# A hybrid attention and expert-retrieval layer on one core: gate rows two units later, a low half ahead of the norm's constants, and another order of loads, copies and factors where the dense experts change stage

## The chip, the cores and the metric

The kernel runs on one core of one Trainium2 chip. The metric is the device time in microseconds of one execution. Before the change the median of three runs is 1756.65 us (1754.71 to 1765.33). Engines are named as the profile names them: PE is TensorE (matrix products), PEld its weight loads, DVE is VectorE, ACT is ScalarE, POOL is GpSimd, SP is SyncE, which here only issues transfers.

## What is computed

One decoder layer on 512 tokens of 1024 features, in float32. The first part is the mixer, the second an expert layer that retrieves 16 of 16384 single-neuron experts for each token and each of 8 heads.

```python
h = rmsnorm(x, norm_mix_g)
proj = h @ w_in                       # all branches at once
o_a = gla_chunked(gq, gk, gv, log_a)  # gated linear attention
o_a = rmsnorm(o_a, gla_norm_g) * silu(gr)
o_b = swa_sink_attention(q, k, sv, attn_sinks)   # window 128, sinks
merged = sigmoid(gate_a) * (o_a @ w_branch_a) + sigmoid(gate_b) * (o_b @ w_branch_b)
x = x + merged @ w_out
xn = rmsnorm(x, norm_ffn_g)
# product keys: top 16 of 128 on each side, top 16 of their sums -> idx, gate (softmax)
out = x + sum_k gate[k] * gelu(peer_u[idx[k]] . xn) * peer_v[idx[k]]
```

## The kernel before

**Weights come as units.** A stream (class Stream, L124 to L183) brings one 128 x 1024 float32 block at a time: SyncE loads it (`raw`, L143), ScalarE makes a rounded high half (`whi`, L162), VectorE or GpSimd makes the low half (`wlo`, L172). Each product is three matmuls (high by high, high by low, low by high), at L231 and L248 in the first part. The first two blocks are split in halves of 512 columns (`first`, L154 and L155) between the rows of the first norm's input (L270 to L276); the third is split by the first call of `get`, which stands behind the constants of the attention (masks and scaled gains, L306 to L330).

**The front.** Units of the mixer follow one another: keys and values of the window attention, queries, then eight units `gr` (swish gate of branch A, L609 to L626) and eight units `gb`. The window attention itself runs as a side generator, one step each few matmuls of the units (`swa`, L428 to L515): scores on TensorE, masks and maxima on VectorE, exponentials on ScalarE, then transposes, and two masked copies `pc` and `pp` (L475, L479) that the products `o_` (L489) read. In the gate units, `gr_act(d)` (L600) puts a tanh of row d on a list that the next attention step hands to ScalarE (L601), and `gr_late` (L604) at the end of the next unit issues the product of that row on VectorE (L609). Row 3 is the first for which this is done in its own unit; rows 0, 1 and 2 are handled together with rows 3, 4 and 5.

**The dense experts.** Instead of gathering, 368 of the 512 tokens go through all 16384 experts, 128 per unit, in three stages of 92, 20 and 16 units (PHASES, L79; main loop L1529 to L1591). Each stage has an up part and a down part. In the up part, `h_step` (L1375) multiplies a block of U into a PSUM bank `hp` (24 matmuls at L231) and ScalarE writes its gelu (L1393) into `ring` or, where it is spilled to memory, `hw`. In the down part, `v_step` multiplies blocks of V into eight accumulators (L1445). Its other operand is the gelu times a gate tile: `w_a` (L1419) multiplies ring and gate tile `gt` on VectorE (`wr`, L1424) and rounds on ScalarE (`wh`, L1429); `w_b` (L1432) makes the low half (`wl`, L1435). The first pair of a stage is made before the last up unit, together with the first half of the second pair. The gate tiles are loaded by `g_load` (L1408) in two pieces: `gd`, built with one-hot matmuls during the first up part, and `g3`, into which 128 scatters of GpSimd (L1143) add the gates of one quarter of the tokens. The first two `g_load` of the kernel are issued by GpSimd in unit 86, the others by SyncE.

**The rest of the tokens.** 144 tokens are handled by gathering rows of U and V: GpSimd gathers one row per token (L1310), VectorE makes the product with the token (L1325), ScalarE its gelu and gate (L1281, L1282), VectorE adds the scaled row of V (L1342). This is a generator (`gather`, L1287); `pump` (L1478) advances it when the planner's counters `pe`, `dve`, `dma` and `pool`, which add a cost per instruction issued, leave room. Up to unit 83 it uses single row buffers ("early"); after `late[0]` is set it uses the pair buffers of the gate builder, and the activation of a row is issued right behind its product. In unit 86 the early rows are used up (L1545), the memory of the routing stage is closed, and the gate loads are issued.

**Banks.** PSUM has eight banks: S2 (two), PT, O, M0 to M3. BANKS (L1527) says which accumulator lies where; up units from 92 on alternate between M0 and M1. Between a down part and the next up part, `sum_phase` (L1490) copies accumulators 7 and 6 on ScalarE (L1502 in the first, L1499 in the second) and leaves the others to the following up units.

The order on every engine is the order in the program: each engine works through its own instructions in turn and waits on semaphores.

Of the kernel before, what the change touches and what calls it, by code (L numbers as in the profile page):

```python
# [47 lines left out]
N0 = 92  # L48
# [4 lines left out]
TAIL = 5  # L53
SLACK = 3.0
DUTY = 0.97
LAND = 10.0
POOLQ = 9.0
# [26 lines left out]
def tile_block(ctx, tc, xT, wst, smalls, wgk2, keysT, uT, vv, uv_rows, out):  # L84
# [186 lines left out]
    for kb in range(KB):  # L271
        g = S("gmix")[:, kb:kb + 1]
        nc.scalar.activation(hhi[:, kb], xt[:, kb], AF.Copy, scale=g)
        nc.vector.scalar_tensor_tensor(hlo[:, kb], xt[:, kb], g, hhi[:, kb].bitcast(F32), OP.mult, OP.subtract)
        if kb < 4:
            st.first(kb // 2, kb % 2)  # L276
    xs = Bt[:, 0]
    rb = F.tile([128, T], F32, name="rb", tag="rb")
    rt = F.tile([128, 4, NT], F32, name="rt")[:, 0:2]
# [320 lines left out]
    def gr_act(d):  # L600
        fill.append(lambda: nc.scalar.activation(gb[:, d], gr[:, d], AF.Tanh, scale=0.5))  # L601
        late.append(d)
# [8 lines left out]
    for d in range(8):  # L611
        w = unit("gr")
        if d == NR:
            flush()
            gb = F.tile([128, KB, T], F32, name="gb", tag="gb")
            side.append(swa())
            nm[0] = 3
            st.defer = True
        ps = proj(w, H, each=tick)
        nc.vector.tensor_tensor(gr[:, d], ps, rb, OP.mult)  # L620
        gr_late()
        if d >= NR:
            gr_act(d)
            if d < 2 * NR:
                gr_act(d - NR)
    for d in range(8):  # L626
        w = unit("gb")
        zero_fill()
# [638 lines left out]
            yield  # L1267

    late, early, used, acc2 = [False], [0], [-1], []
    nxt, born, end, en = [], {}, [False], [0]  # L1270
    sel = XP.tile([128, XG], F32, name="sel")
    nc.gpsimd.tensor_tensor(sel, ident[:, 0:XG], ident[:, XG:2 * XG], OP.add)
# [14 lines left out]
    def gather():  # L1287
# [7 lines left out]

        def issue(k):
            nonlocal grp, n
            while n < min(n_, k + (3 if late[0] else 2) + 2 * end[0]):
                for i in range(min(2 if late[0] else 1, n_ - n)):
                    if late[0]:  # L1300
                        if i == 0:
# [47 lines left out]

        issue(0)  # L1350
        pu, pv = 0, 0
        nxt[:] = [0]
        yield
        while pv < n_:
# [123 lines left out]
    def pump():  # L1478
        for x in (dve, dma, pool):
            x[0] = max(x[0], pe[0] - SLACK)  # L1480
        for _ in range(2):
            if side and max(dve[0], dma[0], pool[0] - (0 if late[0] else POOLQ)) < pe[0] + SLACK:
                if nxt and not late[0] and pe[0] < born[nxt[0]] + LAND:
                    break
                u = used[0]
                step()
                if used[0] > u:
                    break
# [35 lines left out]
                    nc.sync.dma_start(out[(t + 1) * 128 - n:(t + 1) * 128, ch], xr[0:n, t, ch])  # L1524
        return tr

    BANKS = ("S2", "S2", "PT", "O", "M2", "M3", "M0", "M1")  # L1527
    b_s = NB
    for ph, (b0, b1) in enumerate(PHASES):  # L1529
        for b in range(b0, b1):  # L1530
            if b == b1 - 1:
                w_a(b0 // 2)
                w_b(b0 // 2)
                w_a(b0 // 2 + 1)
            h_step(b, feed if LEAD <= b < N0 - GL else None)
            if b == RS[0]:
# [2 lines left out]
                next(r_)  # L1539
            if b == RS[-1]:  # L1540
                side.append(gather())
            if b == N0 - TAIL - 4:
                late[0] = True
            if b == N0 - TAIL - 1:
                while early[0]:  # L1545
                    step()
# [3 lines left out]
            if b == N0 - GL:  # L1550
                assert next(r_, 0) == 0
                while gout:
                    gout.pop(0)()
                g_load(0, nc.gpsimd)
                g_load(1, nc.gpsimd)
            pool[0] = max(pool[0], pe[0] - SLACK)
            if scs:
                b_s = min(b_s, b)
# [13 lines left out]
        for b in range(b0, b1 - 2 if last else b1):  # L1572
# [8 lines left out]
            if b % 2 == 0 and p + 1 < b1 // 2:  # L1581
                w_b(p + 1)
            v_step(b, b == b0, b == b1 - 1)
            pump()
            if b == NB - 6:
                xr = P.tile([128, 4, D], F32, name="xr", tag="hhi")
                nc.sync.dma_start(xr[0:TB, 1], x1s[XG:, 1])
                nc.sync.dma_start(xr[0:XG, 0], x1s[0:XG, 1])
                nc.sync.dma_start(xr[:, 2:4], x1s[:, 2:4])
        if not last:  # L1590
            sum_phase(ph)  # L1591
    wl_ = [get("V", NB - 2), get("V", NB - 1)]
    trs = []
    for c in range(7, -1, -1):
# [89 lines left out]
```

## Time and profile before

| what | value |
|---|---|
| runs (three), median | 1756.65 us |
| lowest, highest | 1754.71, 1765.33 us |
| profiled execution, its own time | 1764.95 us |
| its span, first to last instruction | 1763.0 us |
| mean granted clock of TensorE | 0.992 |
| HBM read, written | 379.67 MB, 42.47 MB |
| first up part begins, ends (PE) | 647.5, 1080.8 us |
| first down part begins, ends | 1083.9, 1455.5 us |
| second up part begins; second down part | 1460.1; 1542.4 us |
| third up part begins; third down part | 1622.9; 1687.5 us |

The profile is one execution. Its rows give a start in us from the span's start, a duration in us, the engine, the line, the operation and its operands (out<-in), and in brackets the idle time before it and what ended it. In the view of waits a row gives an engine's line, whom it waited for, the total, the number of times and the longest. In the view of windows the columns are PE, PEld, DVE, ACT and POOL busy time with instruction counts, then granted clock, DMA share and GB/s.

### The profile page before, as it was taken

The page shows a single profiled execution, that of the slowest core. Times are in us where ns is not written, and L with a number is a line of the kernel's source. Part 1 is how long each engine was busy: PE and PEld are TensorE (multiplying, and loading weights), DVE is VectorE, ACT ScalarE, POOL GpSimd, SP SyncE. Part 2 cuts the span into 40 slices and gives each one's busy share as a digit, 9 for nine tenths or more (in the row PEclk, how much of TensorE's full clock was granted, in tenths as well). Part 3 has the DMA queues.
Part 4 walks back from the last instruction along what each step waited for, and adds up shares of the span by engine and source line. Part 5 has one row for each costly group of instructions (what it writes and reads, how often), then busy time and mean ns, then how long its engine had stood idle before and what let it go on. Part 6 is the DMA issues. An engine that isn't in the chain of part 4 may idle for free.

```text
span 1763.0 us, 26377 instructions
## 1 busy us (share of the span) xinstructions
PE 1724.8 (98%) x9866; PEld 1599.9 (91%) x9866; DVE 1304.9 (74%) x2547; ACT 765.9 (43%) x1334; POOL 705.9 (40%) x447
## 2 busy tenths in 40 slices
PE   9999999999998999999999999999999998999998
PEld 7776688988886889999999989999999998999998
DVE  7767624346337996977778746999889998899874
ACT  5545523335244234355555533444444434444441
POOL 0004444445544451778788872222122223233200
PEclk9999999999998999999999999999999999999999
DMA  4214522222234234699999998999999999999963
GB/s 171 96 60 120 166 98 84 84 72 83 90 129 152 79 104 142 137 267 248 278 290 301 294 304 328 412 412 407 408 404 398 371 386 349 401 377 388 378 244 107
DMA packets 163231, 423.88 MB, mean 240 GB/s; under 512 B 34704, under 2 KB 80144, under 8 KB 144288
## 3 DMA queue, kind: packets, MB, share of 16 engines
q1 hardware_dynamic: 118432, 256.06, 41.9%
q0 software_dynamic: 39488, 152.59, 24.3%
q10 hardware_dynamic: 5184, 13.57, 2.1%
q8 instruction: 77, 1.26, 0.3%
q14 instruction: 50, 0.41, 0.1%
HBM read 379.67 MB, written 42.47 MB: 239 GB/s over the span
## 4 chain that ended last, share of the span: by engine, by line
PE 73%; DMA 8%; DVE 7%; POOL 6%; issue 4%; ACT 2%; SPq 0%; DVEq 0%; POOLq 0%; ACTq 0%
PE oa L1445 21%; PE mm L231 18%; PE hp L231 15%; PE oacc L1445 7%; PE mm L248 6%; POOL g L1143 5%; DMA g<-w,addr 2%; DMA rows<-in_uv_rows_dram,misc 2%; DMA row<-in_uv_rows_dram,misc 2%; DMA gt<-g 1%; POOL row L1310 1%; PE sc L977 1%; PE gp L1188 1%; DVE stt L456 1%; DMA raw<-in_uT_dram 1%
## 5 line engine op out<-in xcount | busy, mean ns | idle before, releaser
L162 ACT CAST whi<-raw 128x1024 fp32r<-128x1024 f32 x347 | 361.6, 1045 | 134.9 <-PE mm L231 26.7
L172 DVE TENSOR_TENSOR wlo<-raw,whi 128x1024 fp32r<-128x1024 f32 x266 | 324.4, 1220 | 58.7 <-ACT whi L162 18.8
L231 PE MATMUL hp<-xh,whi 128*128 128x368 f32 x1024 | 345.1, 337 | 10.2 <-ACT hw L1393 5.7
L1310 POOL DMA_INDIRECT rows<-in_uv_rows_dram,misc x118 | 163.5, 1385 | 454.8 <-DVE accv L1342 381.1
L231 PE MATMUL hp<-xh,wlo 128*128 128x368 f32 x1024 | 339.4, 331 | 0.8 <-DVE wlo L172 0.8
L231 PE MATMUL hp<-xl,whi 128*128 128x368 f32 x1024 | 338.8, 331 | 0.0
L1143 POOL DMA_INDIRECT g<-w,addr x128 | 247.4, 1933 | 95.3 <-issue 43.9
L172 POOL TENSOR_TENSOR wlo<-raw,whi 128x1024 fp32r<-128x1024 f32 x81 | 198.5, 2456 | 156.5 <-ACT whi L162 152.5
L1445 PE MATMUL oa<-wl,whi 128*128 128x368 f32 x768 | 254.0, 331 | 0.0
L1445 PE MATMUL oa<-wh,whi 128*128 128x368 f32 x768 | 253.8, 330 | 0.0
L1445 PE MATMUL oa<-wh,wlo 128*128 128x368 f32 x768 | 253.6, 330 | 0.0
L231 PEld LDWEIGHTS hp<-xh,whi 128*128 128x128 f32 x1024 | 194.1, 190 | 11.9 <-ACT hw L1393 7.1
L231 PEld LDWEIGHTS hp<-xh,wlo 128*128 128x128 f32 x1024 | 193.9, 189 | 1.4 <-DVE wlo L172 1.4
L231 PEld LDWEIGHTS hp<-xl,whi 128*128 128x128 f32 x1024 | 194.2, 190 | 0.0
L1445 PEld LDWEIGHTS oa<-wh,whi 128*128 128x128 f32 x768 | 144.8, 189 | 0.0
L1445 PEld LDWEIGHTS oa<-wh,wlo 128*128 128x128 f32 x768 | 144.8, 189 | 0.0
L1445 PEld LDWEIGHTS oa<-wl,whi 128*128 128x128 f32 x768 | 144.7, 188 | 0.0
L1342 DVE SCALAR_TENSOR_TENSOR accv<-rows,misc,accv 128x1024 f32<-128x1024 f32 x102 | 130.7, 1281 | 15.9 <-ACT misc L1282 15.9
L1325 DVE SCALAR_TENSOR_TENSOR rows<-rows,xtok 128x1024 f32<-128x1024 f32 x102 | 124.6, 1221 | 5.7 <-DMA rows<-in_uv_rows_dram,misc 5.6
L1281 ACT ACTIVATE misc<-misc 128x1 f32<-128x1 f32 x144 | 29.4, 204 | 224.7 <-DVE rows L1325 176.4
L231 PE MATMUL mm<-hhi,whi 128*128 128x512 f32 x256 | 104.1, 406 | 0.0
L231 PE MATMUL mm<-hhi,wlo 128*128 128x512 f32 x256 | 100.0, 391 | 0.0
(593 smaller groups left out, 3300.0 us busy)
## 6 DMA issues: line engine op xcount, KB each, us to landing
raw<-in_uT_dram SPq DMA_DIRECT2D x128, 512.0 KB, 5.2
raw<-in_vv_dram SPq DMA_DIRECT2D x128, 512.0 KB, 8.6
raw<-in_wst_dram SPq DMA_DIRECT2D x92, 512.0 KB, 3.5
gt<-gd SPq DMA_DIRECT2D x30, 480.0 KB, 8.6
gd<-gbuild SPq DMA_DIRECT2D x56, 256.0 KB, 6.7
hs<-hw ACTq DMA_DIRECT2D x36, 368.0 KB, 5.3
ring<-hs SPq DMA_DIRECT2D x36, 368.0 KB
g<-zero SPq DMA_DIRECT2D x16, 512.0 KB, 5.7
```

What stands on the lines that cost most here:

```text
L162: nc.scalar.copy(hi, self.raw[u])
L172: self.lo_eng(u).tensor_tensor(lo, r, hi.bitcast(F32), OP.subtract)
L231: nc.tensor.matmul(ps[:, :n], a[:, kb, :], b[:, kb, c0:c0 + n], start=(kb == 0 and i == 0), stop=(kb == KB - 1 and i == 2))
L248: nc.tensor.matmul(banks[t], a[:, kb, t * 128:(t + 1) * 128], b[:, k, :], start=(first and k == 0 and i == 0), stop=(last and k == kk - 1 ...
L456: nc.vector.tensor_reduce(nm, m, AX.X, OP.max, negate=True)
L977: nc.tensor.matmul(sc[:, t], qp[:, t * 128:(t + 1) * 128], ky[hp], start=True, stop=True)
L1143: i = nc.gpsimd.indirect_dma_start(out=g3, out_offset=bass.IndirectOffsetOnAxis(ap=addr[:, c:c + 1], axis=0), in_=w3[:, c:c + 1], in_offse ...
L1281: nc.scalar.activation(h, h, AF.Gelu)
L1310: nc.gpsimd.indirect_dma_start(out=rows[n], out_offset=None, in_=uv_rows, in_offset=bass.IndirectOffsetOnAxis(ap=ix[:, slots[n][1]:slots[n ...
L1325: nc.vector.scalar_tensor_tensor(cur, cur, 1.0, xs_[kind][0:m, :], OP.mult, OP.mult, accum_out=hc)
L1342: nc.vector.scalar_tensor_tensor(a_, cur, h_[0:m, s_:s_ + 1], a_, OP.mult, OP.add)
L1445: nc.tensor.matmul(accs[c][:, 0:TD], v_[:, cs], a, start=(first and i == 0), stop=(last and i == 2))
```

## The change

- In the front, the third block is split (high half on ScalarE, low half on VectorE) behind row 5 of the norm's input, ahead of rows 6 and 7 and of the constants.
- The gate rows 0, 1 and 2 are handled together with rows 5, 6 and 7 instead of 3, 4 and 5.
- In unit 81 instead of 83, `late` is set, and with it a new flag `held`: as long as it stands no row is gathered, and `pump` only uses up the early rows. In unit 86, behind the two gate loads on GpSimd, the flag falls and the next rows are gathered.
- Accumulators 6 and 7 exchange their banks: 6 lies in M1, 7 in M0.
- In the second and third stage the first factor pair (`w_a` and `w_b`) is made before the last but one up unit; the first half of the second pair stays before the last.
- `sum_phase` is called behind the last `v_step` of a stage, ahead of the last `pump`, no longer behind it.

```diff
         if kb < 4:
             st.first(kb // 2, kb % 2)
+        elif kb == 5:
+            st.splits(3)
...
             gr_act(d)
-            if d < 2 * NR:
-                gr_act(d - NR)
+            if d >= NR + 2:
+                gr_act(d - NR - 2)
...
+    held, more = [False], []
...
-            while n < min(n_, k + (3 if late[0] else 2) + 2 * end[0]):
+            while not held[0] and n < min(n_, k + (3 if late[0] else 2) + 2 * end[0]):
...
         pu, pv = 0, 0
+        more.append(lambda: issue(pv))
...
-            if side and max(dve[0], dma[0], pool[0] - (0 if late[0] else POOLQ)) < pe[0] + SLACK:
+            if side and (early[0] or not held[0]) and max(dve[0], dma[0], pool[0] - (0 if late[0] else POOLQ)) < pe[0] + SLACK:
...
-    BANKS = ("S2", "S2", "PT", "O", "M2", "M3", "M0", "M1")
+    BANKS = ("S2", "S2", "PT", "O", "M2", "M3", "M1", "M0")
...
-            if b == b1 - 1:
+            if b == b1 - (2 if ph else 1):
                 w_a(b0 // 2)
                 w_b(b0 // 2)
+            if b == b1 - 1:
                 w_a(b0 // 2 + 1)
...
-            if b == N0 - TAIL - 4:
-                late[0] = True
+            if b == N0 - TAIL - 6:
+                late[0] = held[0] = True
...
                 g_load(0, nc.gpsimd)
                 g_load(1, nc.gpsimd)
+                held[0] = False
+                more[0]()
...
             v_step(b, b == b0, b == b1 - 1)
+            if b == b1 - 1 and not last:
+                sum_phase(ph)
             pump()
...
-        if not last:
-            sum_phase(ph)
```

## The prediction

> **What bounds the kernel now.** I read the page first (busy shares, chain), then the waits of TensorE, then the timelines of single engines around each wait.
>
> ```profile
> PE 1724.8 (98%) x9866; PEld 1599.9 (91%) x9866; DVE 1304.9 (74%) x2547; ACT 765.9 (43%) x1334; POOL 705.9 (40%) x447
> ...
> PE 73%; DMA 8%; DVE 7%; POOL 6%; issue 4%; ACT 2%; SPq 0%; DVEq 0%; POOLq 0%; ACTq 0%
> ```
>
> TensorE is busy for 1724.8 of 1763.0 us, so a change that takes no matmul away can win at most the idle 38 us and what slow matmuls after idle stretches cost. The waits of TensorE say whose work it missed (total us, times, longest):
>
> ```profile
> PE hp L231 <- ACT hw L1393: 5.7, 4, 3.0
> ...
> PE hp L231 <- ACT yT L1502: 4.5, 1, 4.5
> PE oacc L1445 <- ACT wh L1429: 3.5, 2, 3.1
> ...
> PE mm L248 <- DVE wlo L172: 1.6, 1, 1.6
> ...
> PE oacc L1445 <- DVE wl L1435: 1.0, 2, 0.5
> ```
>
> The last four are places that the diff edits; the first (5.7 us, in the first up stage) is not, since no edit acts before unit 81 of that stage and the instructions up to unit 86 keep their order.
>
> **Part 1, the third low half (front).** ACT, DVE and PE rows, in this order:
>
> ```profile
> 16.12 1.04 ACT L162 CAST whi<-raw 128x1024 fp32r<-128x1024 f32 x1
> ...
> 16.96 0.22 DVE L307 TENSOR_SCALAR mcur<-jp 128x128 uint32<-128x128 int32 x1
> ...
> 18.61 1.22 DVE L172 TENSOR_TENSOR wlo<-raw,whi 128x1024 fp32r<-128x1024 f32 x1
> ...
> 23.08 3.07 DVE L288 TENSOR_TENSOR Bt<-Bt,xsq 128x512 f32<-128x512 f32 x4
> ...
> 19.88 0.50 PE L248 MATMUL mm<-wlo,hhi 128*128 128x512 f32 x1 [1.59 <-DVE wlo L172]
> ...
> 27.72 0.95 PE L295 MATMUL sst<-ones,Bt 128*128 128x1 f32 x8
> ```
>
> VectorE makes the constants from 16.96 to 18.61 and only then this low half; TensorE wanted it at 19.88 - 1.59 = 18.29. After the change it stands ahead of the constants and of the last two norm rows. When the raw weights land is not shown; the cast began at 16.12 without a wait, so at the latest then. That bounds the low half's end: at the latest 16.12 + 1.04 + 1.22 = 18.4, 0.1 late. At the earliest there is no wait. Late next: the last norm rows, 1.0 us later on ScalarE and 1.2 on VectorE; their readers come a whole unit later (4 token tiles x 2 rows x 3 matmuls), so that is hidden. VectorE has the same work in sum, so the sum of squares still ends at 23.08 + 3.07 = 26.15, and TensorE now comes to it at 27.72 - 1.59 = 26.13: some 0.2 us are given back. Gain 1.4 us (bounds 0 and 1.6: if the raw tile lands as late as 16.12, the squares slip too).
>
> **Part 2, the gate rows.** ACT, DVE and PE rows:
>
> ```profile
> 119.30 1.15 ACT L601 ACTIVATE gb<-gr 128x512 f32<-128x512 f32 x2
> ...
> 131.24 1.84 DVE L609 SCALAR_TENSOR_TENSOR gr<-gb,gr 128x512 f32<-128x512 f32 x2
> ...
> 164.06 1.27 DVE L609 SCALAR_TENSOR_TENSOR gr<-gb,gr 128x512 f32<-128x512 f32 x1
> ...
> 126.26 0.65 PE L489 MATMUL o__1137<-pc,sv 128*64 128x256 f32 x4 [1.40 <-DVE pc L475]
> 133.73 0.65 PE L489 MATMUL o__1197<-pc,sv 128*64 128x256 f32 x4 [1.33 <-DVE pc L475]
> 141.13 0.65 PE L489 MATMUL o__1251<-pc,sv 128*64 128x256 f32 x4 [1.45 <-DVE pc L475]
> 153.56 0.65 PE L489 MATMUL o__1360<-pc,sv 128*64 128x256 f32 x4 [0.60 <-DVE pc L475]
> ```
>
> Rows 0, 1, 2 ride with rows 3, 4, 5 now, and with 5, 6, 7 after. So the pairs of tanh and product stand in units 5 to 7 instead of 3 to 5. The first wait hangs on ScalarE, whose tanh pair (1.15) delays the chain of the softmax: one tanh less is 0.55 us. The second and third hang on VectorE, where the pair (1.84) stands right ahead of pc: a single one is 1.27, so 0.57 us each. The fourth has a pair before and after. Two later places get a pair that they had not. What that costs no row shows; the bounds are 0 and the 0.60 of the fourth row, which is such a place with a pair; I take 0.25 each, because singles there wait for nothing. Sum 0.55 + 0.57 + 0.57 - 0.5 = 1.2 us (bounds 0.5 and 1.7).
>
> **Part 3, hold and loads ahead of gathers.** Following the planner's counters with its own costs through both versions: no row is issued between units 81 and 86 in either, so the hold by itself moves nothing. What moves is GpSimd's queue at unit 86: now four row gathers and then the two pairs of gate-tile loads; after, the loads first. GpSimd, VectorE and TensorE rows, then three groups of DMA issues (KB, median us to landing):
>
> ```profile
> 1057.46 1.43 POOL L1310 DMA_INDIRECT rows<-in_uv_rows_dram,misc  x1 [0.30 <-ACT misc L1282]
> ...
> 1062.74 1.00 POOL L1310 DMA_INDIRECT rows<-in_uv_rows_dram,misc  x1 [0.30 <-issue]
> 1063.74 0.62 POOL L1410 DMA_DIRECT2D gt<-gd  x1
> ...
> 1081.29 0.63 DVE L1424 TENSOR_TENSOR wr<-ring,gt 128x448 f32<-128x448 f32 x1 [7.24 <-DMA gt<-gd]
> ...
> 1083.92 0.44 PE L1445 MATMUL oacc<-wh,whi 128*128 128x368 f32 x1 [3.14 <-ACT wh L1429]
> ...
> 1085.49 0.48 PE L1445 MATMUL oacc<-wl,whi 128*128 128x368 f32 x1
> ...
> 1088.83 0.38 PE L1445 MATMUL oa<-wh,whi 128*128 128x368 f32 x1
> ...
> gt<-gd SPq DMA_DIRECT2D x30, 480.0 KB, 8.6
> ...
> rows<-in_uv_rows_dram,misc POOLq DMA_INDIRECT x118, 9.7
> ...
> gt<-gd POOLq DMA_DIRECT2D x2, 480.0 KB, 19.6
> ```
> ```profile
> 1100.00:1200.00 100.00, 100.00 (x600) 100.00 (x599) 91.83 (x116) 44.17 (x74) 24.23 (x17) 1.00 1.02 412
> ```
>
> The loads that GpSimd issues behind the gathers take 19.6 us, the thirty that SyncE issues 8.6. VectorE waits for them to 1081.29, and TensorE, which ended the up stage at 1083.92 - 3.14 = 1080.78, starts 2.63 after that. Undisturbed, TensorE starts 600 matmuls in 100 us, 0.167 each (second fence: TensorE busy 100.00, 600 matmuls). From 1085.49 to 1088.83 eleven starts take 0.304 each: 11 x 0.137 = 1.5 us lost to a slow clock. The wait costs 3.14 + 0.5 (the wl row of the waits) + 1.5 = 5.1.
>
> After: the loads issue between 1057.46 (where the first gather stands) and 1063.74 (if they still wait for the last scatter or for memory of the early rows), landing 8.6 later at 1066 to 1072. They are needed by 1080.78 - 2.63 = 1078.2, so the cover is 6 us. Late next is nothing but TensorE itself; I leave 0.2. Gain 4.9 (bounds 0, if they take 19.6 wherever they stand, and 5.1). Queued behind the loads: the four gathers, up to 8.8 us later (1063.74 + 4 x 0.62 - 1057.46), read first in the down stage; see the last rival.
>
> [...]
>
> **Part 4, copies ahead of the pump, banks 6 and 7 exchanged.** At the end of the first down stage, ACT rows and then PE rows:
>
> ```profile
> 1454.57 1.03 ACT L162 CAST whi<-raw 128x1024 fp32r<-128x1024 f32 x1
> 1458.76 0.20 ACT L1281 ACTIVATE misc<-misc 128x1 f32<-128x1 f32 x1 [3.16 <-DVE rows L1325]
> ...
> 1459.20 0.81 ACT L1502 COPY yT<-oa 128x368 f32<-128x368 f32 x2
> ...
> 1460.06 0.68 PE L231 MATMUL hp<-xh,whi 128*128 128x368 f32 x1 [4.53 <-ACT yT L1502]
> ...
> 1464.22 0.42 PE L231 MATMUL hp<-xl,whi 128*128 128x368 f32 x1
> ```
>
> ScalarE stands 3.16 us at the gelu of a row whose product VectorE has not made, with the copies that free the banks queued behind it. After, the copies follow the cast, which ends at 1455.60; accumulator 7, whose copy comes first, lies in bank M0, which up unit 92 wants, so one copy (half of 0.81) frees it: 1456.0, and 0.1 for the hand-over (1460.06 less 1459.20 + 0.81). TensorE stopped at 1460.06 - 4.53 = 1455.53: 0.6 of the 4.53 stay. The slow starts go too: 13 starts in 4.16 us from 1460.06 to 1464.22, 13 x 0.153 = 2.0. Gain 4.5 - 0.6 + 2.0 = 5.9 (bounds 3.3, if the cast waited for its weights as long as the gelu now does, so that half of wait and clock stays, and 6.5). What moves behind the copies is the gelu of one row; its addition waits 0.8 longer, hidden by the two rows that are gathered in advance. The same edit in the second change from down to up finds no wait to remove.
>
> **Part 5, first factor pair one unit earlier (second and third stage).**
>
> ```profile
> 1687.47 0.44 PE L1445 MATMUL oacc<-wh,whi 128*128 128x368 f32 x1 [0.40 <-ACT wh L1429]
> 1688.42 0.43 PE L1445 MATMUL oacc<-wl,whi 128*128 128x368 f32 x1 [0.52 <-DVE wl L1435]
> ```
>
> These two waits, 0.9 us, go; the pair is ready a unit of 24 x 0.167 = 4.0 us sooner. The second stage has no such wait now; it would have one if VectorE fell behind there, and the edit covers that. Its cost: VectorE's low half of a later unit slips by the pair's 2.6 us (the 2.63 above) and is read 4 us or more later: hidden. Gain 0.9 (bounds 0 and 0.9).
>
> **Sum.** 1.4 + 1.2 + 4.9 + 5.9 + 0.9 = 14.3 us. The profiled run took 1764.95 (span 1763.0 and 1.95 around it), 8.3 above the median 1756.65 of the three runs (1754.71 to 1765.33). Against its own time: 1764.95 - 14.3 = 1750.7. I carry the gain to the median: **1742.4 us**. What differs between these executions no row shows, which is the widest doubt here.
>
> **Rivals.** (a) *The transfers are the bound in the dense stages, and the waits come back elsewhere.* For: from 1100 to 1200 the DMA share is 1.02 at 412 GB/s. Against: TensorE is at 100.00 in the same row, so transfers keep up without help from a stall. Only the front's gain stays: 1756.65 - 2.6 = 1754. Chance 0.13. [...]
>
> (b) *The gate tiles land late wherever they stand*, because the whole memory traffic of the change sets it: part 3 gives nothing, 1742.4 + 4.9 = 1747.3. For: 19.6 against 8.6 could be the time of day, not the order. Against: 4 MB of gathers stand ahead of them in the same queue. Chance 0.13.
>
> (c) *More than forecast.* The waits for hw (5.7) fall in the first up stage. In an execution without them TensorE reaches the change of stages 5.7 sooner while the gate tiles keep their hour on GpSimd's queue, so that the wait of part 3 is 5.7 longer, and all of it goes: 1742.4 - 5.7 = 1736.7. Against: the scatters ahead may then be sooner too. Chance 0.20.
>
> (d) *Slower.* The four gathers, 8.8 later, land late: with 9.7 from 1066.2 the first lands at 1076, but with the 19.6 of a crowded queue at 1086. Its product stands on VectorE ahead of the second factor pair and a low half (about 6 us with its addition), wanted two units into the down stage, 1080.8 + 8.0 = 1088.8. So from a landing at 1083 on TensorE waits: 3 us each time at 1086, and 1.5 of slow clock. It must recur for the two pairs in flight over two more turns, 4 x 4.5 = 18, to outweigh 14.3: 1742.4 + 18 = 1760. Chance 0.04, since two rows are held in advance and catch up.
>
> **From cases to numbers.** Forecast 0.50, with its own range 1738 to 1748. The range 1733 to 1755 takes in (a), (b) and (c) with the bounds of the parts. A measurement of this kernel tells about 1% (17.6 us: below 1739.1, above 1774.2) from no change. Faster by over 1%: 0.17 of (c) and 0.08 of the forecast, 0.25. Slower by over 1%: 0.02, half of (d). Within: 0.73.
>
> **What would show it.** Right: no wait of hp for yT over 1 us; no wait of the first oacc for wh in the first down stage, and the POOL loads landing in about 9 us; no wait at 19.88; three pc waits near 0.85, 0.75 and 0.9. Wrong: DVE idle for gt as long as now, rows' products waiting for DMA at the start of the down stage, or the clock below 1.00 after the changes of stage.

## The result, and the profile after

The median of the changed kernel is 1747.22 us (17 runs, 1741.99 to 1759.73), that of the kernel before beside it 1756.65 (17 runs, 1748.69 to 1769.48): ratio 0.9937, 95% interval 0.9912 to 0.9961. The kernel became about 9 us faster, which is within 1%. The forecast was 1742.4. The profiled execution took 1749.61 us, span 1747.5; the sum in the prediction had put it at 1750.7. Here and below, a ratio that has an interval need not equal that of the two medians beside it.

The page after, TensorE's share and the chain; then the waits of TensorE that are new or that the prediction spoke of (total us, times, longest):

```profile
PE 1717.4 (98%) x9866; PEld 1593.2 (91%) x9866; DVE 1305.4 (75%) x2547; ACT 767.5 (44%) x1334; POOL 709.6 (41%) x447
...
PE 69%; DVE 9%; DMA 9%; POOL 6%; issue 4%; ACT 3%; DVEq 0%; SPq 0%; ACTq 0%; POOLq 0%
```
```profile
PE hp L231 <- ACT hw L1397: 4.0, 2, 2.5
PE oa L1449 <- ACT ring L1397: 2.5, 2, 1.9
PE o__1540 L491 <- DVE pc L477: 1.4, 1, 1.4
...
PE hp L231 <- ACT yT L1506: 0.5, 1, 0.5
```

The wait for `yT` fell from 4.5 to 0.5, those of the accumulators for `wh` and `wl` are gone, and two kinds stand there that the kernel before did not have: accumulators that wait for the gelu of the last up unit (`ring`), and a later `pc`.

**Stage by stage.** The first matmul of each stage in the timeline of PE cuts the span into stretches that can be compared (us; a wait at the head of a stage counts to the stretch before it; the table ahead of the prediction has 647.5 for the start of the first up part and 1622.9 for the third, the rows have 647.26 and 1622.70):

| stretch | before | after | after less before |
|---|---|---|---|
| start to first up stage | 647.26 | 645.84 | -1.42 |
| first up stage, with the wait at its end | 436.66 | 429.27 | -7.39 |
| first down stage, with the wait at its end | 376.14 | 369.66 | -6.48 |
| second up stage, with the wait at its end | 82.34 | 80.36 | -1.98 |
| second down stage to the last matmul | 216.84 | 218.58 | +1.74 |

Of the 7.39 only 3.14 are the wait at the end of the stage. The other 4.25 lie inside the first up stage: waits that sum to 4.9 instead of 6.5 us, and TensorE busy for 424.6 instead of 427.0 us with the same matmuls. Over the fourteen profiled executions in this document, that stage without its final wait lasts 423.6 to 437.9 us, in an order that does not follow the edits (before 433.5, after 429.3, the changed kernel once more 434.4). The waits come in the same few units, 41 to 57, 76 to 80 and 84 to 86, most of them for ScalarE; only the last of these units lie behind unit 81, where the edits begin, and the profiles of e2, e7 and e10 have no wait in this stage. That is what differs between executions, which the prediction had to leave open; what delays ScalarE there was not followed. The first down stage, on the other hand, is 369.64 to 369.67 us in six of the seven profiles that have the edits at its two ends (369.85 in the seventh, e9, where the wait at its end is 0.70 instead of 0.5). Without that wait it is 369.15: 2208 matmuls of 0.1672, TensorE alone.

**The front.** DVE and PE rows, and one of POOL:

```profile
15.21 1.23 DVE L172 TENSOR_TENSOR wlo<-raw,whi 128x1024 fp32r<-128x1024 f32 x1
16.36 1.41 DVE L274 SCALAR_TENSOR_TENSOR hlo<-xt,sm,hhi 128x512 fp32r<-128x512 f32 x2
17.68 0.22 DVE L309 TENSOR_SCALAR mcur<-jp 128x128 uint32<-128x128 int32 x1
...
25.91 0.95 PE L297 MATMUL sst<-ones,Bt 128*128 128x1 f32 x8
...
123.97 0.65 PE L491 MATMUL o__1135<-pc,sv 128*64 128x256 f32 x4 [0.88 <-DVE pc L477]
130.84 0.65 PE L491 MATMUL o__1193<-pc,sv 128*64 128x256 f32 x4 [0.73 <-DVE pc L477]
137.73 0.65 PE L491 MATMUL o__1247<-pc,sv 128*64 128x256 f32 x4 [0.96 <-DVE pc L477]
150.47 0.65 PE L491 MATMUL o__1357<-pc,sv 128*64 128x256 f32 x4 [0.91 <-DVE pc L477]
163.48 0.65 PE L491 MATMUL o__1483<-pc,sv 128*64 128x256 f32 x4 [0.15 <-DVE pc L477]
...
168.09 2.11 DVE L611 SCALAR_TENSOR_TENSOR gr<-gb,gr 128x512 f32<-128x512 f32 x2
...
168.32 1.33 POOL L467 TENSOR_TENSOR p__1451<-p__1451,stt 128x512 f32<-128x512 f32 x1 [2.64 <-DVE stt L466]
...
170.12 0.68 DVE L634 TENSOR_TENSOR gb<-mm,rb 128x512 f32<-128x512 f32 x1
170.72 0.68 DVE L477 TENSOR_TENSOR pc<-pt,fcur 128x512 f32<-128x512 f32 x1
...
171.45 0.65 PE L491 MATMUL o__1540<-pc,sv 128*64 128x256 f32 x4 [1.44 <-DVE pc L477]
```

The low half is made at 15.21, ahead of the constants, and TensorE comes to the sum of squares at 25.91 instead of 27.72: 1.81 sooner, 1.4 forecast. The first three waits for `pc` are 0.88, 0.73 and 0.96 (forecast 0.85, 0.75, 0.9). But the fourth grew from 0.60 to 0.91, and of the two new places one costs 0.15 and the other 1.44: there the pair of products (2.11) and the first product of the `gb` units stand ahead of `pc` on VectorE. The waits sum to 5.07, before to 4.78.

**First change from up to down.** POOL, DVE and PE rows, then the group of DMA issues (KB, median us to landing), then the window in which the down stage begins (busy time and count of PE, PEld, DVE, ACT, POOL; granted clock, DMA share, GB/s):

```profile
1058.92 0.61 POOL L1414 DMA_DIRECT2D gt<-gd  x1 [5.78 <-issue]
...
1061.54 1.01 POOL L1313 DMA_INDIRECT rows<-in_uv_rows_dram,misc  x1 [0.30 <-ACT whi L162]
...
1068.45 0.99 DVE L1428 TENSOR_TENSOR wr<-ring,gt 128x448 f32<-128x448 f32 x2
...
1075.11 0.34 PE L1449 MATMUL oacc<-wh,whi 128*128 128x368 f32 x1
...
gt<-gd POOLq DMA_DIRECT2D x2, 480.0 KB, 8.6
```
```profile
1070.00:1080.00 10.00, 10.00 (x62) 10.00 (x61) 6.69 (x10) 3.92 (x8) 0.00 (x0) 1.00 1.01 419
```

The group's landing is that of one of its two loads, the only one that each trace holds: 8.6 us instead of 19.6. The tile is there before VectorE wants it, and TensorE enters the down stage without a wait and at full clock.

**First change from down to up, and the second and third from up to down.** ACT and PE rows:

```profile
1444.26 0.83 ACT L1506 COPY yT<-oa 128x368 f32<-128x368 f32 x2
1444.77 0.44 PE L231 MATMUL hp<-xh,whi 128*128 128x368 f32 x1 [0.51 <-ACT yT L1506]
...
1528.97 0.43 PE L1449 MATMUL oa<-wh,whi 128*128 128x368 f32 x1 [0.65 <-ACT ring L1397]
...
1672.62 0.20 ACT L1284 ACTIVATE misc<-misc 128x1 f32<-128x1 f32 x1 [3.14 <-DVE rows L1328]
1672.86 0.30 ACT L1285 ACTIVATE misc<-misc 128x1 f32<-128x1 f32 x1
1673.53 0.81 ACT L1433 CAST wh<-wr 128x736 fp32r<-128x736 f32 x1 [0.37 <-DVE wr L1428]
1674.24 1.04 ACT L162 CAST whi<-raw 128x1024 fp32r<-128x1024 f32 x1
1675.19 0.47 ACT L1397 ACTIVATE ring<-hp 128x368 f32<-128x368 f32 x1
1675.71 0.44 PE L1449 MATMUL oa<-wh,whi 128*128 128x368 f32 x1 [1.89 <-ACT ring L1397]
```

The wait of 4.53 is 0.51 (0.6 forecast). The waits for the first pair are gone, but in their place TensorE waits 0.65 and 1.89 us for a gelu: accumulator 6 lies in M1 now, the bank of the last up unit, and ScalarE comes to that unit's gelu late, because it stood 3.14 us at a row's gelu whose product VectorE had not made, with two casts behind that (the rows are those of the third stage; ScalarE stood as long at 1525.89 in the second).

### The profile page after: what moved, and what is told of

Read it like the earlier page. It is cut to its first block, busy times and chain, and to the rows that moved or that the text cites. A ratio compares the mean times of both kernels' runs of the same rounds, so it can differ in the third digit from the quotient of the medians.

```text
span 1747.5 us, 26380 instructions
## 1 busy us (share of the span) xinstructions
PE 1717.4 (98%) x9866; PEld 1593.2 (91%) x9866; DVE 1305.4 (75%) x2547; ACT 767.5 (44%) x1334; POOL 709.6 (41%) x447
## 4 chain that ended last, share of the span: by engine, by line
PE 69%; DVE 9%; DMA 9%; POOL 6%; issue 4%; ACT 3%; DVEq 0%; SPq 0%; ACTq 0%; POOLq 0%
PE oa L1449 21%; PE mm L231 18%; PE hp L231 10%; PE oacc L1449 7%; PE mm L248 6%; POOL g L1145 4%; DMA rows<-in_uv_rows_dram,misc 4%; DMA g<-w,addr 2%; DMA row<-in_uv_rows_dram,misc 1%; PE gp L1190 1%; DMA raw<-in_uT_dram 1%; DVE wlo L172 1%; PE sc L979 1%; DVE accv L1345 1%; POOL row L1313 1%
## 5 line engine op out<-in xcount | busy, mean ns | idle before, releaser
L1145 POOL DMA_INDIRECT g<-w,addr x128 | 253.0, 1976 | 89.1 <-issue 41.8
```

Source lines behind the costliest of these rows:

```text
L1145: i = nc.gpsimd.indirect_dma_start(out=g3, out_offset=bass.IndirectOffsetOnAxis(ap=addr[:, c:c + 1], axis=0), in_=w3[:, c:c + 1], in_offse ...
```

## The experiments

The theory after the first comparison: the copies ahead of the pump are the main gain; the order of loads and gathers wins what the execution at hand would have waited; the exchange of the banks and the earlier pair give part of it back in new waits behind ScalarE. The rival: the terms of the prediction hold as they are, and what is missing in the median is the spread of the executions. A first group took the edits one by one into the kernel before.

**e1_loads_first**: the kernel before with the hold and the loads ahead of the gathers, and nothing else.

```diff
-            if b == N0 - TAIL - 4:
-                late[0] = True
+            if b == N0 - TAIL - 6:
+                late[0] = held[0] = True
...
                 g_load(1, nc.gpsimd)
+                held[0] = False
+                more[0]()
```

> The kernel before with the hold and the gate-tile loads ahead of the gathers alone. My theory (the order on GpSimd's queue sets when the gate tiles land): the two POOL loads land in about 8.6 us instead of 19.6, TensorE's wait for wh at the first change from up to down (3.14 and 0.5 us before) is under 0.3 and the slow starts behind it go, so that the first down stage starts some 3.5 us sooner behind the end of the up stage; the wait of hp for yT (4.5) stays. Time 4 to 6 us under the kernel before. Rival (the traffic sets the landing wherever the loads stand): landing near 19 us, the wait stays above 2.5, time within 1 us of the kernel before.

Median 1754.81 us (10 runs) against 1756.15 (25 runs), ratio 0.9993 [0.9959, 1.0026]. In the profile the wait for `wh` and `wl` and the slow start at the first down stage are gone (from 1070 to 1090 the granted clock is 1.00 and TensorE busy throughout). The other change of stage is as before, PE and ACT rows:

```profile
1445.77 0.20 ACT L1282 ACTIVATE misc<-misc 128x1 f32<-128x1 f32 x1 [3.58 <-DVE rows L1326]
...
1446.20 0.81 ACT L1504 COPY yT<-oa 128x368 f32<-128x368 f32 x2
...
1447.07 0.67 PE L231 MATMUL hp<-xh,whi 128*128 128x368 f32 x1 [4.95 <-ACT yT L1504]
```

In the profile the order does what it was to do. The time was expected 4 to 6 us lower; the interval of about 6 us on either side cannot tell a gain of 0 from one of 5.

**e2_copies_first**: the kernel before, with `sum_phase` ahead of the last pump.

```diff
             v_step(b, b == b0, b == b1 - 1)
+            if b == b1 - 1 and not last:
+                sum_phase(ph)
             pump()
...
-        if not last:
-            sum_phase(ph)
```

> The kernel before with sum_phase ahead of the last pump alone, banks 6 and 7 as they were. My theory: the wait of hp for yT falls from 4.5 us to about 1.0 (end of the cast plus two copies of 0.41 and 0.1), and the clock stays at 1.00 in the window behind it; 3.5 us and 2.0 us of slow starts, 5.5 in all. Rival (transfers bound the dense stages, and a wait taken away comes back): new waits of hp for wlo or of ACT for raw weights in the second up stage that sum to 3 us or more, time within 2 us of the kernel before. The wait at the first change from up to down stays at 3 us or so in both.

Median 1748.47 (10 runs), ratio 0.9946 [0.9909, 0.9983]: a gain of 3 to 16 us, in which both the 5.5 that this edit was expected to bring and the whole of the change have room. A DVE row at the first change from up to down, then PE and DVE rows at the later ones:

```profile
1067.47 0.63 DVE L1424 TENSOR_TENSOR wr<-ring,gt 128x448 f32<-128x448 f32 x1 [2.79 <-DMA gt<-gd]
...
1441.97 0.44 PE L231 MATMUL hp<-xh,whi 128*128 128x368 f32 x1 [1.14 <-ACT yT L1502]
...
1519.00 1.23 DVE L1325 SCALAR_TENSOR_TENSOR rows<-rows,xtok 128x1024 f32<-128x1024 f32 x1 [3.42 <-DMA rows<-in_uv_rows_dram,misc]
...
1523.94 0.99 DVE L1424 TENSOR_TENSOR wr<-ring,gt 128x448 f32<-128x448 f32 x2
...
1525.82 0.67 PE L1445 MATMUL oacc<-wh,whi 128*128 128x368 f32 x1 [3.31 <-ACT wh L1429]
```

With the banks as they were, 1.14 of the wait for `yT` stays. The second change from up to down, which waited for nothing in the profile of before, now waits 3.31 for the first pair: VectorE stood 3.42 us at a gathered row that had not landed, and the pair's product at 1523.94 comes behind that row and the next. In the full change the pair is made a unit sooner, and no profile with it waits there for `wh`. And although the gathers stand ahead of the loads here, TensorE does not wait at the first change; the expectation had said 3 us, so the wait there is not the kernel's alone.

**e3_banks_only**: the kernel before with accumulators 6 and 7 exchanged (one profile).

```diff
-    BANKS = ("S2", "S2", "PT", "O", "M2", "M3", "M0", "M1")
+    BANKS = ("S2", "S2", "PT", "O", "M2", "M3", "M1", "M0")
```

> The kernel before with banks 6 and 7 exchanged alone. My theory: the wait of hp for yT is one copy shorter (4.5 to about 4.1), no more, since the copies still stand behind a gelu that waits for VectorE. At the changes from up to down the accumulator that lies in M1 is now wanted 3 matmuls (0.5 us) sooner after the start of the down stage, while ScalarE's gelu of the last up unit is not sooner: with the late starts of this kernel (it waits for wh or wl first) I expect no wait for ring, at most 0.3. Rival: the exchange is what made the waits for ring (0.65 and 1.89 in the changed kernel); then they show here with about the same size.

1767.68 us. The wait for `yT` is 3.72, no accumulator waits for a gelu, and the waits for the pair stay (1.67 and 0.53 at the first change, 0.53 at the second, 0.81 and 0.52 at the third). The exchange by itself moves little while the copies stand behind the pump: 0.8 of the wait for `yT`, 0.4 expected, in one execution.

**e7_gathers_first**: the changed kernel with the gathers ahead of the loads.

```diff
-                g_load(0, nc.gpsimd)
-                g_load(1, nc.gpsimd)
                 held[0] = False
                 more[0]()
+                g_load(0, nc.gpsimd)
+                g_load(1, nc.gpsimd)
```

> The changed kernel with the four row gathers put back ahead of the gate-tile loads in unit 86; hold and everything else as changed. My theory: the loads land 18 us or so after their issue again and the wait of the first oacc for wh is back at 2.5 us or more with slow starts behind it, so 4 to 6 us slower than the changed kernel; the other waits as in the changed kernel. Rival (it was the hold, or the hour, not the order): landing near 9 us, no wait, same time as the changed kernel.

Median 1751.16 (10 runs, 1742.08 to 1764.33), ratio to before 1.0002 [0.9969, 1.0034]. The wait at the first change is 0.87 and 0.52, not 2.5 or more as the theory said: a miss in its size. Of the time the runs say less: the two medians by themselves give a ratio of 0.9972, so that the loss against the changed kernel is some 4 us by the medians and 11 by the ratios.

A second group took one part of the change back, one profile each; the kernel before took 1760.54 beside them.

**e4_banks_back** (the exchange undone), **e5_pair_back** (the first pair again behind the last but one up unit), **e6_gates_back** (the gate rows as before) and **e9_gates_one** (gate rows 0, 1 and 2 one unit later instead of two):

```diff
e5  -            if b == b1 - (2 if ph else 1):
    +            if b == b1 - 1:
e6  -            if d >= NR + 2:
    -                gr_act(d - NR - 2)
    +            if d < 2 * NR:
    +                gr_act(d - NR)
e9  -            if d >= NR + 2:
    -                gr_act(d - NR - 2)
    +            if NR + 1 <= d <= NR + 3:
    +                gr_act(d - NR - 1)
```

> The changed kernel with banks 6 and 7 as they were before. My theory (the new waits of oa for ring come from two things together: the down stage now starts at once, and accumulator 6 in M1 is wanted 0.5 us sooner, while the gelu of the last up unit stands on ScalarE behind the second wh): the waits for ring fall by 0.5 each, from 0.65 to about 0.15 and from 1.89 to about 1.4, and the wait of hp for yT grows from 0.51 to about 0.9. Rival (the exchange alone makes them): both waits for ring go.

> The changed kernel with the first factor pair of the second and third stage made before the last up unit again. My theory: the second and third down stage start later, held by wh and wl (0.4 and 0.5 us or more at the third, up to 1 us at the second), and the waits for ring shrink by about as much, because the gelu stands where it stood: the sum of the waits for wh, wl and ring at the two changes stays within 1 us of the 2.5 of the changed kernel. Rival (the earlier pair made the gelu late): the waits for ring go and the third change costs 0.9 again, as in the kernel before; 1.6 us less in all.

> The changed kernel with the gate rows 0 to 2 back with rows 3 to 5. My theory from the two traces: the first three pc waits are again 1.40, 1.33 and 1.45 and the fourth 0.60, and the new ones of the changed kernel (0.15 and 1.44) are gone, so that the gate units end within 0.3 us of where the changed kernel ends them (4.8 us of waits against 4.8): moving the rows by two units was worth nothing. Rival (it was worth the 1.2 of the forecast): the stages behind the gate units start 1 us or more later than in the changed kernel.

> The changed kernel with the gate rows 0 to 2 put with rows 4 to 6, one unit later than before instead of two. My theory (a pair in front of pc costs where VectorE is behind, and the place behind row 7, where the product of the first gb unit joins the pair, is the dear one, 1.44): the waits are about 0.88, 0.75, 1.45, 0.9, 0.15 and none behind row 7, so the part before the experts ends about 0.7 to 1.3 us sooner than in the changed kernel. Rival (pairs cost the same in sum wherever they stand): it ends within 0.3 us of the changed kernel.

They took 1754.66, 1753.41, 1743.88 and 1751.64 us. Single times say little here (the first up stage alone spans 14 us), so the waits count:

- e4: `yT` 1.86, no wait for a gelu. By this profile the exchange wins 1.35 at this change of stage (1.86 less 0.51), more than the theory's 0.4; by e2, whose banks are also the old ones, 0.6 (1.14 less 0.51).
- e5: no wait for a gelu, but 0.46 at the second change for `wl` and 0.44 and 0.53 at the third for the pair, 1.43 in sum against 2.54 in the changed kernel's profile.
- e6: the waits for `pc` are 1.41, 1.34, 1.47 and 0.61 as before, none is new, and the sum, 4.83, is below the changed kernel's 5.07. Two units later is worth nothing, as the theory said, and perhaps less: the first up stage begins at 644.95 here, and at 645.27 to 646.62 in the seven profiles with the rows two units later and the new front.
- e9: 0.88, 0.73, 2.08, 0.32 and 0.18, sum 4.19. The third is 0.6 above its forecast and the fourth 0.6 below; the sum is 0.6 below that of the kernel before. The first up stage begins at 644.50, and in e10 below, which has the same gate rows, at 644.94.

The last group ran on one chip, with the changed kernel among them.

**e12_after_again**, the changed kernel unaltered, and **e11_no_hold**, the changed kernel without the hold (`late` in unit 83 again), so that the gathers are ahead of the loads as before:

```diff
e11  -            if b == N0 - TAIL - 6:
     -                late[0] = held[0] = True
     +            if b == N0 - TAIL - 4:
     +                late[0] = True
     ...
     -                held[0] = False
     -                more[0]()
```

> The changed kernel itself, for the comparisons with the other three on the same chip. Theory (the length of the first up stage is not the kernel's but the execution's): its first up stage differs from 429.3 us by up to 6, the waits for the gelu's tile sum to 1 to 3.5 us, the wait of hp for yT is 0.4 to 0.8, and the ratio to the kernel before is 0.992 to 0.997. Rival (the first execution was typical in all): the stage is 429 within 1 us and the waits are 0.65 and 1.89 within 0.2.

> The changed kernel without the hold, so that the four gathers stand ahead of the gate-tile loads again, as in the kernel before. Theory (the wait at the first change from up to down is 0 to 5 us by the execution, as e1_loads_first and e2_copies_first showed, so the order of loads and gathers is worth 0 to 2 us in a median): the wait there for wh and wl sums to 0 to 2.5 in this profile, and the median is 0 to 2 us above the changed kernel's. Rival (the forecast's term): the wait is about 3.7 and the median 4 to 5 us above.

The changed kernel: 1750.86 (12 runs), ratio to before 0.9954 [0.9927, 0.998]. Without the hold: 1757.54 (12 runs), 0.9979 [0.9951, 1.0008]. The medians differ by 6.7 us and the means by 5.7 (95% interval 1.4 to 9.9 by resampling the single times): this order has a worth of its own, and my theory's 0 to 2 is probably too low, though the interval still touches it. The profile of e11 shows it, POOL, DVE and PE rows and the window:

```profile
1056.75 0.62 POOL L1412 DMA_DIRECT2D gt<-gd  x1
...
1073.54 0.63 DVE L1426 TENSOR_TENSOR wr<-ring,gt 128x448 f32<-128x448 f32 x1 [7.30 <-DMA gt<-gd]
...
1076.19 0.68 PE L1447 MATMUL oacc<-wh,whi 128*128 128x368 f32 x1 [3.21 <-ACT wh L1431]
```
```profile
1070.00:1080.00 10.00, 6.50 (x28) 5.81 (x27) 4.92 (x7) 2.77 (x4) 0.00 (x0) 0.76 0.64 250
```

Here the wait and the slow start of before are back.

One thing more lies in the traces of e7 and e11: in both, every engine has the same instructions, on the same tiles and shapes, in the same order. So the two are in effect one program, and the hold by itself moves nothing, as the prediction said. What sets them apart from the changed kernel is the order of loads and gathers alone. That one program waited 0.87 and 0.52 us at the first change in one execution and 3.21 and 0.29 in another; and on two chips its ratio to before is 1.0002 and 0.9979, where the changed kernel has 0.9937 and 0.9954.

The second profile of the changed kernel brought a surprise of another kind: no accumulator waits for a gelu at all (0.65 and 1.89 in the first). Those waits belong to the execution.

**e8_gelu_first** (on ScalarE the gelu of the last up unit ahead of the cast of the second factor tile, and accumulator 6 last) and **e10_all** (the same, with the gate rows of e9):

```diff
-            if b == b1 - 1:
-                w_a(b0 // 2 + 1)
             h_step(b, feed if LEAD <= b < N0 - GL else None)
+            if b == b1 - 1:
+                w_a(b0 // 2 + 1)
...
-        for c in range(8) if first else range(7, -1, -1):
+        for c in (0, 1, 2, 3, 4, 5, 7, 6) if first else range(7, -1, -1):
```

> The changed kernel with two orders turned round: at the end of an up stage ScalarE makes the gelu of the last up unit before the cast of the second factor tile, and the first down unit takes the accumulator that waits for this gelu last. Theory (the two new waits of TensorE for the gelu's tile, 0.65 and 1.89 us in the changed kernel, come from that cast ahead of the gelu and from the place of accumulator 6): both are at most 0.3, no other wait appears at the three changes from up to down above 0.6, and the time is 1 to 2.5 us below the changed kernel's on the same chip. Rival (the gelu is late because a row's product holds up ScalarE, whatever the order): the waits stay above 0.6 in one place at least and the time is the same within 1 us.

> The kernel of e8_gelu_first, and the gate rows 0, 1, 2 one unit later than before the change instead of two. Theory (sizes add): pc waits sum to about 4.2 us as in e9_gates_one (5.1 in the changed kernel), no wait for the gelu's tile above 0.3, time 2 to 3.5 us below the changed kernel's on the same chip. Rival (what sets the time is the length of the first up stage, which differs by more than 10 us between executions): the median lies within 1.5 us of the changed kernel's, on either side.

e8: 1745.38 (5 runs, 1743.59 to 1750.8), ratio to before 0.9923 [0.9894, 0.9953]. e10: 1744.83 (7 runs, 1741.86 to 1748.71), 0.9931 [0.9902, 0.9959]. Both lie below the changed kernel on the same chip; the means differ by 4.3 (0.5 to 8.0) and 5.0 (1.5 to 8.8). But the theory of the waits isn't borne out. e8's profile has no wait for a gelu, nor has e12's, without that edit; and e10's has one of 0.75, and another at the next change, ACT and PE rows:

```profile
1601.87 0.20 ACT L1284 ACTIVATE misc<-misc 128x1 f32<-128x1 f32 x1 [2.91 <-DVE rows L1328]
1602.10 0.29 ACT L1285 ACTIVATE misc<-misc 128x1 f32<-128x1 f32 x1
1602.30 1.03 ACT L162 CAST whi<-raw 128x1024 fp32r<-128x1024 f32 x1
1603.24 0.82 ACT L1503 COPY ev<-oa 128x368 f32<-128x368 f32 x2
1603.75 0.44 PE L231 MATMUL hp<-xh,whi 128*128 128x368 f32 x1 [2.00 <-ACT ev L1503]
```

The pattern is that of `yT` before the change: ScalarE stands 2.91 us at a row's gelu, and the copies that free the banks come behind it. The rival in e8's expectation, that a row's product holds ScalarE whatever the order, fits e10's profile, but neither e8's, where no such wait is left, nor the times, which it had put within 1 us of the changed kernel's. The rival in e10's, a median within 1.5 us of the changed kernel's, falls too: it is 6.0 below. What makes e8 and e10 faster in the median stays open; they are the fastest versions tried, and what e9's gate rows save in `pc` waits (0.9) is the only part of it that a profile shows.

## Why the prediction was right where it was, and where it was not

The forecast was a gain of 14.3 us and a time that moves by less than 1%; the measured gain is 9.4, so the time lies 4.8 above the forecast, inside its range. It lies on the number of rival (b), 1747.3, which had the loads gain nothing. That is chance: their gain did come, and the shortfall is spread over parts 1 and 2, 3 and 5. Point by point, with what the profiles of all kernels give (a kernel that lacks an edit stands for before, one that has it for after):

| part | forecast | profile before to after | over the profiles |
|---|---|---|---|
| 1 and 2, front and gate rows | 2.6 | 1.4 | 1.1 |
| 3, loads ahead of gathers | 4.9 | 5.6 | 3.4 (0.4 to 6.3) |
| 4, copies first, banks | 5.9 | 6.0 | 5.8 (5.5 to 6.0) |
| 5, earlier pair, and the new waits | 0.9 | -1.7 | -1.5 (-4.0 to 0.8) |
| sum | 14.3 | 11.3 | 8.8 |

In the last column, parts 1 and 2 are the mean start of the first up stage in four profiles without the new front and gate rows (647.16) less that in seven with both (646.05); part 4 is the mean over before, e1 and e3 of the wait above 0.5 and of the second up stage above 80.37; parts 3 and 5 are worked out below. Each of these means rests on three to seven executions, so that the sum is an estimate.

The 11.3 and the 4.25 of the first up stage make the 15.5 between the two spans. The 8.8 stands beside 9.4 between the medians of the first comparison and 8.7 between those of e12 and its kernel before; an agreement this close is partly luck. So the profiled execution came out near its forecast, 1749.61 for 1750.7, partly by the luck of its first up stage; the median shows the true size.

**Part 1 held.** 1.81 sooner at the sum of squares (1.32 in e12, at 26.40), for 1.4. Over all profiles, four with the old front and ten with the new one, the mean is 27.93 against 26.09, so 1.8.

**Part 2 failed** at "I take 0.25 each, because singles there wait for nothing". The sum of 1.2 came out as -0.3 (4.78 to 5.07). The fourth place, said to be the same before and after, cost 0.31 more, and one of the two new places cost 1.44, far past the 0.60 that was to bound it: `pc` there has the first product of a `gb` unit ahead of it as well, and the pair itself took 2.11 instead of 1.84, with a product on GpSimd (168.32) in the same time. A single product there is hidden, a pair is not. e6 confirms it from the other side.

**Part 3 was right in mechanism, and its size is the one of a single execution.** In the kernels with the gathers first, the loads are issued 16 to 17 us before TensorE ends the up stage (17.0 before, 17.0 in e2 and e7, 16.2 in e11), and the chain behind them takes 2.63, so that they have about 14 us. Behind the four gathers VectorE has the tile after 17.6 us (before), 16.8 (e11), 14.6 (e3), 14.5 (e7) and 13.2 (e2); ahead of them TensorE did not wait in any of nine profiles. The five losses, each the wait and what the down stage without its own wait for `yT` is longer than 369.15, are in the same order 5.6, 6.3, 2.8, 2.0 and 0.4, in the mean 3.4. The prediction took the first of them for the typical one. The times of e7 and e11 against the changed kernel put the part higher, at 4 to 11 us by the four pairs of their ratios; the profiles do not show where the rest would lie. Rival (c), a longer wait where the up stage is shorter, falls: at 423.6 us (e2) the loss is the smallest, and at 427.4 (e11) the largest. Rival (b) falls with the landing of 8.6 and with the runs of e7 and e11.

**Part 4 held in both its terms.** 4.53 to 0.51 is 4.02 of wait (3.9 forecast); the slow starts after it are the 1.98 by which the second up stage got shorter (2.0 forecast). Of the wait, e4 puts 1.35 on the exchange of the banks, and e2 0.6.

**Part 5 failed** at its lower bound of 0: the two waits it names went, but the bound leaves no room for new ones. That accumulator 6 would lie in the bank of the last up unit and wait for its gelu is in the list of banks, and was not followed. And the copies at the second change from down to up, where "the same edit finds no wait to remove", do not stay without a wait once TensorE comes sooner: 0.16 to 2.16 us for `ev` in seven of nine profiles that have these edits, none in the five that lack the copies first or the earlier pair. In the six profiles with the changed stage ends (after, e6, e7, e9, e11, e12) these waits sum to 2.54, 0.73, 2.31, 4.95, 3.98 and 0.16, mean 2.45; in before, e1 and e3, which have the old ones, 0.92, 0 and 1.86, mean 0.93. The difference is the -1.5. Measured by the stretch from the second down stage to the last matmul, which takes in the slow matmuls behind these waits, it is -2.2 (219.1 against 216.9). The wait for the gelu stands in six of the eight profiles that have both the exchange and the earlier pair, and in none of the six that lack one of them, e4 and e5 among these. So each of the two edits seems to be needed for it; but e12 has both and no such wait, so a single profile does not prove it. Taken back, each brings a wait of its own again, and no profile here shows a better choice.

**Rival (a)**, the transfers as the bound: with 1.01 of DMA share and 419 GB/s, TensorE ran through the first down stage at 0.1672 us a matmul without a gap. It falls. **Rival (d)**: no row's product made TensorE wait at the start of the first down stage in any profile with the loads first.

## What to carry to other kernels

A stall that is removed at a change of stage shows the next one in the same queue: here ScalarE, in order, stood at a row's gelu in three different places (3.16 us ahead of `yT` before, 3.14 ahead of `ring` after, 2.91 ahead of `ev` in e10), VectorE at a row that had not landed in a fourth (3.42 ahead of `wh` in e2), and the edits moved the casualty. So follow every instruction behind the one that blocks, and every bank that an exchange gives a new neighbour. And a wait that one profile shows against a deadline with a margin near zero (14 us of cover for landings of 13 to 18) is a draw, not a term: price it by a range of executions, or carry half of it.

## What the runs showed of the hardware

The length of a wait alone does not tell whether the clock of TensorE fell. At a change of stage it fell at each of the longer waits: 3.14 and 4.53 us before, 4.95 in e1, 3.31 in e2, 3.21 in e11, and 3.72 in e3 by its second up stage of 82.66. Among shorter ones it went either way: after a wait of 2.43 in e5 the first matmul takes 0.67 us, after one of 2.48 in the profile after 0.43, both in the first up stage:

```profile
917.19 0.67 PE L231 MATMUL hp<-xh,wlo 128*128 128x368 f32 x1 [2.43 <-DVE wlo L172]
```
```profile
1050.90 0.43 PE L231 MATMUL hp<-xh,whi 128*128 128x368 f32 x1 [2.48 <-ACT hw L1397]
```

In the traces of before and after, the granted clock reads 1.00 or 0.50, and the times at which it changes in one trace lie whole multiples of 3.41 us apart; idle time is counted here in steps of that length. In the dense stages before, the clock falls at 1054.80, 1085.52 and 1457.57, behind steps with 2.88, 2.34 and 2.04 us idle; the longest idle time in a step with no fall behind it is 1.32 us there. In the profile after, where the wait of 2.48 is split over two steps with 1.37 and 1.11 us idle, the clock does not fall once in the dense stages. In e11 a wait of 1.82 is followed by matmuls of 0.51 us instead of 0.33, from 1682.82 to 1685.88, and one of 2.16, at 1612.27, is not. The windows are a step of e7, in which its wait of 1.96 lies whole, the step behind it, and the step of e10 that holds 1.62 of a wait of 2.00, with no slow matmul behind it:

```profile
1603.20:1606.61 3.41, 1.45 (x9) 1.39 (x9) 3.41 (x5) 3.12 (x6) 0.70 (x1) 1.00 0.37 155
1606.61:1610.02 3.41, 3.41 (x13) 3.41 (x12) 2.21 (x5) 0.00 (x0) 2.71 (x2) 0.50 1.01 306
```
```profile
1602.13:1605.54 3.41, 1.79 (x11) 1.79 (x12) 3.41 (x4) 2.88 (x5) 1.11 (x1) 1.00 0.61 255
```

The falls at 1054.80 and 1085.52 before last one step each, with 0.11 and 0.00 us idle in it; that at 1457.57, at the wait of 4.53, lasts two, with 2.49 us idle in the first. By the rows in the prediction, the step from 1085.52 costs 1.5 us of matmuls (eleven starts of 0.304 us instead of 0.167). One earlier fall, in the mixer of e2, stands behind a step with 1.52 us idle, less than the 1.62 of e10, so that no limit can be read from these numbers.

The slow starts cost 1.3 to 2.3 us each time at the second up stage (81.68 in e1, 82.34 in before, 82.66 in e3, against 80.36).

The one load on GpSimd's queue whose landing the trace holds took 19.6 us behind four gathers and 8.6 ahead of them. The difference of 11.0 is close to an estimate for the bytes of those gathers (4 x 128 rows of memory of 8 KB, 4.2 MB) at the 412 GB/s of the dense stages, 10.2 us. It is one execution of each: ahead of the gathers the same load took 3.7 to 3.9 us in e4 and e5 and 8.3 in e6, and behind them VectorE had the tile after 13.2 to 17.6 us.
